# An adapter-merged linear layer: opening load ahead of the barrier, a held chunk, deeper turning, and set-up tensors inside a data buffer

## The chip, the cores and the metric

The kernel runs on one core of a Trainium2 chip. The metric is the device time of one launch in microseconds; the median of several runs is given. A profile of one execution shows what each engine did.

## What is computed

```python
x_flat = x.reshape(-1, in_dim)          # 32768 x 256, fp32
y = x_flat @ W                          # W: 256 x 256
lora_out = x_flat @ lora_A              # 256 x 16
lora_out = lora_out * lora_E            # 16
lora_out = lora_out @ lora_B            # 16 x 256
y = y + scale * lora_out
```

x and the output are 32 MB each. The low-rank part is merged into the weights once, so that per row of x there is one product with a 256 x 256 matrix.

## The kernel before

x is cut into 8 chunks of 4 MB. A chunk has 128 partitions with 32 rows of x on each, and sits in one of six buffers ("homes") in the on-chip memory. Results overwrite the x they come from, and the home is then stored. Chunks 6 and 7 reuse homes 0 and 1, so their loads (line 104, the wait in `load`) wait until chunks 0 and 1 are stored.

A chunk has 8 groups of 4 rows per partition; there are 64 groups, numbered through. Each passes these engines:

- GpSimd casts x to bf16 into `stage` (line 151), two buffers. It waits for the chunk's load where a chunk or piece begins, and for the turn two groups earlier.
- PE transposes the group in `turn` (line 196): pairs of bf16 are moved as fp32 words, four instructions a group, into `psum_xt`.
- ScalarE copies the turned x to `xt` (line 162), two buffers.
- PE multiplies by the merged weights in `multiply` (line 204), eight instructions a group, into `psum_y`.
- VectorE evicts `psum_y` to the home (line 181). After the last group of a chunk it signals that the chunk is done (line 185).

PE's program is a loop of `turn(i + 1)`, `multiply(i)`: it stands at the turn of the next group before it multiplies this one, so the last group of a chunk is multiplied only when the next chunk's first cast is there.

All transfers are issued by SyncE, in the order written out in `ORDER`: loads of chunks 0 to 5, stores of 0 and 1, loads of 6 and 7, stores of 2 to 7. The engines that move data take the transfers of a queue in this order. Chunk 0 is loaded in three pieces. After the first piece's load SyncE issues the four set-up loads (line 115: W, lora_A, lora_E, lora_B). A tiny store of 2 KB (line 125) goes out once the first group is evicted. Each store waits for its chunk (`s_chunk`). The final wait for the stores (line 238) is appended at the end of SyncE's program.

Set-up: PE transposes lora_A (line 216), VectorE scales it by lora_E into `ate` (line 167), PE multiplies by lora_B (line 222), VectorE adds W and writes `weff` in bf16 (line 177). At entry all engines meet in a barrier before the kernel's own instructions begin.

Of the kernel before, what the change touches and what calls it, by code (L numbers as in the profile page):

```python
# [7 lines left out]
P = 128  # L8
FP32 = mybir.dt.float32
# [6 lines left out]
N_HOMES = 6  # L16
# [6 lines left out]

EARLY_AFTER = 1

CG = 4
GPC = ROWS // CG
N_GROUPS = N_CHUNKS * GPC

NS, NX, NT, NY = 2, 2, 2, 2  # L30

UNROLL = 4

# [2 lines left out]
def kernel(  # L36
# [10 lines left out]
    nc = tc.nc  # L47
# [3 lines left out]
    M = out_flat.shape[1]  # L51
    R = lora_B.shape[0]
    KT = K // P
    assert N == N_CHUNKS * ROWS * P and K == M and KT == 2

    x_chunks = x_flat.rearrange("(c p b) k -> c p b k", p=P, b=ROWS)
    y_chunks = out_flat.rearrange("(c p b) m -> c p b m", p=P, b=ROWS)

    sbuf, psum, sem = nc.alloc_sbuf_tensor, nc.alloc_psum_tensor, tc.alloc_semaphore
    homes = [sbuf(f"home{h}", [P, ROWS, K], FP32) for h in range(N_HOMES)]  # L60
    stage = [sbuf(f"stage{i}", [P, CG, K], BF16) for i in range(NS)]
    xt = [sbuf(f"xt{i}", [P, CG, KT, P], BF16) for i in range(NX)]
    ident = sbuf("ident", [P, P], FP32)

    w_sb = sbuf("w_sb", [P, KT, M], FP32)
    a_sb = sbuf("a_sb", [P, KT, R], FP32)
    b_sb = sbuf("b_sb", [R, M], FP32)
    e_sb = sbuf("e_sb", [R, 1], FP32)
    ate = sbuf("ate", [R, KT, P], FP32)
    weff = sbuf("weff", [P, KT, M], BF16)  # L70
    psum_xt = [psum(f"psum_xt{i}", [P, CG, P], FP32) for i in range(NT)]
    psum_y = [psum(f"psum_y{i}", [P, CG, M], FP32) for i in range(NY)]

    pieces = []
    for c in range(N_CHUNKS):
        s = 0
# [3 lines left out]
    loaded = {pc: sem(f"loaded_{pc[0]}_{pc[1]}") for pc in pieces}  # L80
    set_up_loaded = {n: sem(f"loaded_{n}") for n in ("w", "a", "b", "e")}
    stored_of = {c: sem(f"stored_{c}") for c in range(N_CHUNKS - N_HOMES)}
    stored_rest = nc.alloc_semaphore("stored_rest")
    s_ident = sem("ident_made")
    s_pe_set_up = sem("pe_set_up")
    s_ate = sem("ate_made")
    s_stage = sem("staged")
    s_turned = sem("turned")
    s_xt = sem("xt_made")
    s_y = sem("multiplied")  # L90
    s_free = sem("y_free")
# [4 lines left out]
    def home(c):  # L96
        return homes[c % N_HOMES]

    sync, gpsimd, scalar, vector, tensor = nc.sync, nc.gpsimd, nc.scalar, nc.vector, nc.tensor

    def sync_program():
        def load(pc):
            c, s, e = pc
            if c >= N_HOMES:
                sync.wait_ge(stored_of[c - N_HOMES], 16)
            sync.dma_start(out=home(c)[:, s:e, :], in_=x_chunks[c, :, s:e, :]).then_inc(loaded[pc], 16)

        load(pieces[0])
        for name, to, of in (
            ("w", w_sb, W.rearrange("(q t) m -> q t m", t=KT)),  # L110
            ("a", a_sb, lora_A.rearrange("(q t) r -> q t r", t=KT)),
            ("e", e_sb, lora_E[:, None]),
            ("b", b_sb, lora_B),
        ):
            sync.dma_start(out=to[:], in_=of).then_inc(set_up_loaded[name], 16)
        for step in ORDER:
            c = int(step[1:])
            if step[0] == "L":
                for pc in pieces:
                    if pc[0] == c and pc != pieces[0]:  # L120
                        load(pc)
                if c == EARLY_AFTER:

                    sync.wait_ge(s_first, 1)
                    sync.dma_start(out=y_chunks[0, :16, 0, :32], in_=home(0)[:16, 0, :32]).then_inc(s_early, 16)
            else:
                sync.wait_ge(s_chunk, c + 1)
                if c == 0:
                    sync.wait_ge(s_early, 16)
                sync.dma_start(out=y_chunks[c], in_=home(c)[:]).then_inc(stored_of.get(c, stored_rest), 16)  # L130

    def gpsimd_program():
        gpsimd.memset(ident[:], 0.0).then_inc(s_ident, 1)  # L133
        gpsimd.wait_ge(s_ident, 1)
        gpsimd.affine_select(  # L135
            out=ident[:],
            in_=ident[:],
            compare_op=ALU.not_equal,
            fill=1.0,
            base=0,  # L140
            pattern=[[-1, P]],
            channel_multiplier=1,
        ).then_inc(s_ident, 1)
        for g in range(N_GROUPS):
            c, b = g // GPC, g % GPC * CG
            for pc in pieces:
                if pc[0] == c and pc[1] == b:
                    gpsimd.wait_ge(loaded[pc], 16)
            if g >= NS:
                gpsimd.wait_ge(s_turned, g - NS + 1)  # L150
            gpsimd.tensor_copy(out=stage[g % NS][:], in_=home(c)[:, b:b + CG, :]).then_inc(s_stage, 1)  # L151

        gpsimd.wait_ge(s_turned, N_GROUPS - NS + 1)
        gpsimd.drain().then_inc(s_stage, 1)

    def scalar_program():
        for g in range(N_GROUPS):
            scalar.wait_ge(s_turned, g + 1)
            if g >= NX:
                scalar.wait_ge(s_y, g - NX + 1)  # L160
            halves = psum_xt[g % NT][:].bitcast(BF16).rearrange("q b (p t) -> q b t p", t=KT)
            scalar.copy(out=xt[g % NX][:], in_=halves).then_inc(s_xt, 1)  # L162

    def vector_program():
        vector.wait_ge(set_up_loaded["e"], 16)
        vector.wait_ge(s_pe_set_up, 1)
        vector.tensor_scalar(  # L167
            out=ate[:],
            in0=psum_y[0][:R, :KT, :P],
            scalar1=e_sb[:],  # L170
            scalar2=float(scale),
            op0=ALU.mult,
            op1=ALU.mult,
        ).then_inc(s_ate, 1)
        vector.wait_ge(set_up_loaded["w"], 16)
        vector.wait_ge(s_pe_set_up, 2)
        vector.tensor_add(out=weff[:], in0=w_sb[:], in1=psum_y[1][:, :KT, :]).then_inc(s_free, NY)  # L177
        for g in range(N_GROUPS):
            c, b = g // GPC, g % GPC * CG
            vector.wait_ge(s_y, g + 1)  # L180
            vector.tensor_copy(out=home(c)[:, b:b + CG, :], in_=psum_y[g % NY][:]).then_inc(s_free, 1)  # L181
            if g == 0:
                vector.drain().then_inc(s_first, 1)
            if g % GPC == GPC - 1:
                vector.drain().then_inc(s_chunk, 1)

    def tensor_program():
        def take(s):
            tensor.wait_ge(s, 1).then_inc(s, -1)  # L189

        def turn(i):
            take(s_stage)

            words = stage[i % NS][:].bitcast(FP32)
            for b in range(CG):
                ins = tensor.transpose(psum_xt[i % NT][:, b, :], words[:, b, :], ident[:])  # L196
            ins.then_inc(s_turned, 1)

        def multiply(i):
            take(s_xt)  # L200
            take(s_free)
            for b in range(CG):
                for t in range(KT):
                    ins = tensor.matmul(  # L204
                        psum_y[i % NY][:, b, :],
                        xt[i % NX][:, b, t, :],
                        weff[:, t, :],
                        start=(t == 0),
                        stop=(t == KT - 1),
                    )  # L210
            ins.then_inc(s_y, 1)

        tensor.wait_ge(s_ident, 2)
        tensor.wait_ge(set_up_loaded["a"], 16)
        for t in range(KT):
            ins = tensor.transpose(psum_y[0][:R, t, :P], a_sb[:, t, :], ident[:])  # L216
        ins.then_inc(s_pe_set_up, 1)
        turn(0)
        tensor.wait_ge(set_up_loaded["b"], 16)
        tensor.wait_ge(s_ate, 1)  # L220
        for t in range(KT):
            ins = tensor.matmul(psum_y[1][:, t, :], ate[:, t, :], b_sb[:], start=True, stop=True)  # L222
        ins.then_inc(s_pe_set_up, 1)
        assert N_GROUPS % UNROLL == 0 and all(UNROLL % n == 0 for n in (NS, NX, NT, NY))
        with tensor.Fori(0, N_GROUPS // UNROLL):
            for i in range(UNROLL):
                turn(i + 1)
                multiply(i)

    with tc.tile_critical(no_gpsimd_drain=True):  # L230
        sync_program()
        gpsimd_program()
        scalar_program()
        vector_program()
        tensor_program()

    def wait_for_stores(nc):
        nc.sync.wait_ge(stored_rest, 16 * N_HOMES).then_inc(stored_rest, -16 * N_HOMES)

    nc.at_finalize(wait_for_stores)  # L240


# [33 lines left out]
```

## Time and profile before

| what | value |
|---|---|
| time, median of 3 runs | 163.35 us (163.25 to 163.46) |
| span of the profiled execution | 162.0 us |
| moved | HBM read 33.85 MB, written 33.56 MB, mean 416 GB/s |
| eviction, line 181 | 64 of 1225 ns |
| cast, line 151 | 64 of 1042 ns |
| copy of turned x, line 162 | 64 of 1012 ns |
| a whole load of 4 MB, issue to landing | 19.7 us median |
| a store of 4 MB, issue to landing | 43.3 us median |

The long times from issue to landing are mostly time in the queue behind older transfers. A row of the page that cuts the span into 40 slices shows one slice as about 4 us. Times within the profile count from the first instruction recorded; the device time is 1.3 us longer than the span.

### The profile page before, as it was taken

How to read it: one execution, taken by the hardware profiler on the slowest of the kernel's cores; microseconds unless marked ns; L12 is line 12 of the kernel's file. 1: busy time of each engine (PE TensorE's matmuls, PEld its weight loads, DVE VectorE, ACT ScalarE, POOL GpSimd, SP SyncE). 2: the span in 40 equal slices, each digit the busy share in tenths (PEclk: the TensorE clock that was granted, in tenths of full speed). 3: DMA queues.
4: the chain of work that ended last, by engine and by line, in shares of the span. 5: the costliest groups of instructions: out<-in, count | busy, mean ns of one | idle time of the engine just before them, and what ended most of it. 6: DMA issues, size and time to landing. Idle time of an engine off the chain costs nothing. (4 is left out here: it accounts for less than half of the span.)

```text
span 162.0 us, 2150 instructions
## 1 busy us (share of the span) xinstructions
PE 96.9 (60%) x778; PEld 80.1 (49%) x778; DVE 79.6 (49%) x66; ACT 66.1 (41%) x65; POOL 67.1 (41%) x70
## 2 busy tenths in 40 slices
PE   0399928999999999999900089999960000000000
PEld 0268817888888888888800068888840000000000
DVE  0116854888888888888830017888880000000000
ACT  3044725777767677777700026676720000000000
POOL 1455518777777677777200066677500000000000
PEclk9999999999999999999995558999995555555555
DMA  5999898999999997999999999999999999999992
GB/s 166 419 455 457 388 518 388 388 518 388 388 518 388 388 512 324 461 390 429 469 396 429 469 396 429 455 421 429 445 429 429 445 421 453 421 429 445 421 429 105
DMA packets 2979, 67.43 MB, mean 416 GB/s; under 512 B 528, under 2 KB 544, under 8 KB 672
## 3 DMA queue, kind: packets, MB, share of 16 engines
q1 hardware_dynamic: 2976, 67.41, 97.5%
q14 instruction: 3, 0.02, 0.0%
HBM read 33.85 MB, written 33.56 MB: 416 GB/s over the span
## 5 line engine op out<-in xcount | busy, mean ns | idle before, releaser
L181 DVE COPY home<-psum_y 128x1024 f32<-128x1024 f32 x64 | 78.4, 1225 | 31.9 <-PE psum_y L204 29.9
L151 POOL CAST stage<-home 128x1024 bf16<-128x1024 f32 x64 | 66.4, 1042 | 47.8 <-DMA home<-in_x_dram 26.0
L162 ACT COPY xt<-psum_xt 128x1024 bf16<-128x1024 bf16 x64 | 64.8, 1012 | 51.6 <-PE psum_xt L196 51.6
L204 PE MATMUL psum_y<-weff,xt 128*128 128x256 bf16 x512 | 68.4, 278 | 0.4
L204 PEld LDWEIGHTS psum_y<-weff,xt 128*128 128x128 bf16 x512 | 47.0, 99 | 14.4 <-issue 6.4
L196 PE MATMUL psum_xt<-ident,stage 128*128 128x128 f32 x260 | 41.1, 283 | 16.0 <-PEq L189 16.0
L196 PEld LDWEIGHTS psum_xt<-ident,stage 128*128 128x128 f32 x260 | 31.9, 147 | 18.1 <-issue 17.2
L216 PE MATMUL psum_y<-ident,a_sb 128*16 128x128 f32 x2 | 0.6, 394 | 6.6 <-DMA a_sb<-in_lora_A_dram 6.6
L167 DVE TENSOR_SCALAR ate<-psum_y,e_sb 16x256 f32<-16x256 f32 x1 | 0.5, 472 | 7.3 <-PE psum_y L216 7.3
L216 PEld LDWEIGHTS psum_y<-ident,a_sb 128*16 128x16 f32 x2 | 0.1, 90 | 6.6 <-issue 6.6
L222 PE MATMUL psum_y<-b_sb,ate 16*128 16x256 f32 x4 | 2.1, 670 | 0.0
L177 DVE TENSOR_TENSOR weff<-w_sb,psum_y 128x512 bf16<-128x512 f32 x1 | 0.7, 689 | 2.4 <-PE psum_y L222 2.4
L162 ACT ACT_TABLE_LOAD x1 | 1.3, 1283 | 0.9 <-SPq L230 0.9
L222 PEld LDWEIGHTS psum_y<-b_sb,ate 16*128 16x128 f32 x4 | 1.2, 319 | 0.5 <-issue 0.3
L133 POOL MEMSET ident<- 128x128 f32 x1 | 0.2, 206 | 0.5 <-SPq L230 0.5
L135 POOL TENSOR_SCALAR_AFFINE_SELECT ident<-ident 128x128 f32<-128x128 f32 x1 | 0.3, 293 | 0.2 <-POOL ident L133 0.2
L257 POOL MEMSET const-float32-0.0<- 128x1 f32 x1 | 0.1, 99 | 0.2 <-issue 0.2
L257 POOL MEMSET const-bfloat16-1.0<- 128x1 bf16 x1 | 0.1, 103 | 0.0
L257 POOL MEMSET const-uint8-127<- 128x1 uint8 x1 | 0.1, 103 | 0.0
L257 POOL MEMSET const-float32-1.0<- 128x1 f32 x1 | 0.1, 99 | 0.0
## 6 DMA issues: line engine op xcount, KB each, us to landing
out_dram<-home SPq DMA_DIRECT2D x8, 4096.0 KB, 43.3
home<-in_x_dram SPq DMA_DIRECT2D x7, 4096.0 KB, 19.7
home<-in_x_dram SPq DMA_DIRECT2D x2, 1024.0 KB, 5.0
home<-in_x_dram SPq DMA_DIRECT2D x1, 2048.0 KB, 9.7
w_sb<-in_W_dram SPq DMA_DIRECT2D x1, 256.0 KB, 4.9
a_sb<-in_lora_A_dram SPq DMA_DIRECT2D x1, 16.0 KB, 4.6
e_sb<-in_lora_E_dram SPq DMA_DIRECT2D x1, 0.1 KB, 4.4
b_sb<-in_lora_B_dram SPq DMA_DIRECT2D x1, 16.0 KB, 3.8
```

Source lines behind the costliest of these rows:

```text
L133: gpsimd.memset(ident[:], 0.0).then_inc(s_ident, 1)
L135: gpsimd.affine_select(out=ident[:], in_=ident[:], compare_op=ALU.not_equal, fill=1.0, base=0, pattern=[[-1, P]], channel_multiplier=1,).t ...
L151: gpsimd.tensor_copy(out=stage[g % NS][:], in_=home(c)[:, b:b + CG, :]).then_inc(s_stage, 1)
L162: scalar.copy(out=xt[g % NX][:], in_=halves).then_inc(s_xt, 1)
L167: vector.tensor_scalar(out=ate[:], in0=psum_y[0][:R, :KT, :P], scalar1=e_sb[:], scalar2=float(scale), op0=ALU.mult, op1=ALU.mult,).then_in ...
L177: vector.tensor_add(out=weff[:], in0=w_sb[:], in1=psum_y[1][:, :KT, :]).then_inc(s_free, NY)
L181: vector.tensor_copy(out=home(c)[:, b:b + CG, :], in_=psum_y[g % NY][:]).then_inc(s_free, 1)
L196: ins = tensor.transpose(psum_xt[i % NT][:, b, :], words[:, b, :], ident[:])
L204: ins = tensor.matmul(psum_y[i % NY][:, b, :], xt[i % NX][:, b, t, :], weff[:, t, :], start=(t == 0), stop=(t == KT - 1),)
L216: ins = tensor.transpose(psum_y[0][:R, t, :P], a_sb[:, t, :], ident[:])
L222: ins = tensor.matmul(psum_y[1][:, t, :], ate[:, t, :], b_sb[:], start=True, stop=True)
L257: nc = _bacc.Bacc("TRN2", target_bir_lowering=False, num_devices=1)
```

## The change

It does several things at once:

- The first x load and the load of lora_A are moved, after the program has been built, to the front of SyncE's and ScalarE's instructions, ahead of the entry barrier ("early load").
- The set-up loads are issued by ScalarE instead of SyncE, lora_A first and W last.
- W, lora_B, the scaled transposed lora_A and lora_A lie in the last home, home 5. The load of chunk 5 waits for the merged weights (`s_weff`) before it overwrites them.
- PE turns two groups ahead of the multiplication, with four buffers for turned x in PSUM and four in the on-chip memory.
- GpSimd's first cast of chunk 5 (the sixth chunk) waits until chunks 0 and 1 are stored ("held back as well": chunks 6 and 7 wait for these stores already, through their loads).
- The last signal of GpSimd counts two, for the two turns that run past the end; the callback that appends the final wait is registered earlier in the source.

The aim is to start the transfers sooner, to free memory for the buffers, and to keep compute of chunk 5 away from the first two stores.

```diff
+HELD = N_HOMES - 1
-NS, NX, NT, NY = 2, 2, 2, 2
+NS, NX, NT, NY = 2, 4, 4, 2
...
-    w_sb = sbuf("w_sb", [P, KT, M], FP32)
-    a_sb = sbuf("a_sb", [P, KT, R], FP32)
-    b_sb = sbuf("b_sb", [R, M], FP32)
+    last_home = homes[N_HOMES - 1]
+    w_sb = last_home[:, 0:KT, :]
+    b_sb = last_home[:R, KT, :]
+    ate = last_home[:R, KT + 1, :].rearrange("r (t p) -> r t p", p=P)
+    a_sb = last_home[:, KT + 2, :KT * R].rearrange("q (t r) -> q t r", r=R)
...
+    opening = []
+    def ahead_of_entry_barrier(nc):
+        blocks = nc.main_func.blocks
+        for name in opening:
...
+            first = blocks[0].instructions
+            at = next(
+                n for n, i in enumerate(first) if i.engine == ins.engine and isinstance(i, mybir.InstDrain)
+            )
+            blocks[0].instructions = first[:at] + [ins] + first[at:]
+    nc.at_finalize(ahead_of_entry_barrier)
...
     def sync_program():
         def load(pc):
             c, s, e = pc
+            if c == N_HOMES - 1:
+                sync.wait_ge(s_weff, 1)
...
-        load(pieces[0])
-        for name, to, of in (
...
-            sync.dma_start(out=to[:], in_=of).then_inc(set_up_loaded[name], 16)
+        opening.append(load(pieces[0]).ins.name)
...
+            if (c, b) == (HELD, 0):
+                for held_by in stored_of.values():
+                    gpsimd.wait_ge(held_by, 16)
...
-        gpsimd.drain().then_inc(s_stage, 1)
+        gpsimd.drain().then_inc(s_stage, 2)
...
     def scalar_program():
+        for name, to, of in (
+            ("a", a_sb, lora_A.rearrange("(q t) r -> q t r", t=KT)),
+            ("e", e_sb[:], lora_E[:, None]),
+            ("b", b_sb, lora_B),
+            ("w", w_sb, W.rearrange("(q t) m -> q t m", t=KT)),
+        ):
+            ins = scalar.dma_start(out=to, in_=of).then_inc(set_up_loaded[name], 16)
+            if name == "a":
+                opening.append(ins.ins.name)
...
+        vector.drain().then_inc(s_weff, 1)
...
+        turn(1)
...
             for i in range(UNROLL):
-                turn(i + 1)
+                turn(i + 2)
                 multiply(i)
```

More of the change, by code (lines that the diff above doesn't have):

```diff
@@ L63 @@
     ident = sbuf("ident", [P, P], FP32)
-    w_sb = sbuf("w_sb", [P, KT, M], FP32)
-    a_sb = sbuf("a_sb", [P, KT, R], FP32)
-    b_sb = sbuf("b_sb", [R, M], FP32)
+    last_home = homes[N_HOMES - 1]
[3 more added lines that the diff above has]
+    a_sb = last_home[:, KT + 2, :KT * R].rearrange("q (t r) -> q t r", r=R)
     e_sb = sbuf("e_sb", [R, 1], FP32)
-    ate = sbuf("ate", [R, KT, P], FP32)
     weff = sbuf("weff", [P, KT, M], BF16)
@@ L86 @@
     s_ate = sem("ate_made")
+    s_weff = sem("weff_made")
     s_stage = sem("staged")
@@ L99 @@
     sync, gpsimd, scalar, vector, tensor = nc.sync, nc.gpsimd, nc.scalar, nc.vector, nc.tensor
+    opening = []
+    def ahead_of_entry_barrier(nc):
+        blocks = nc.main_func.blocks
+        for name in opening:
+            block = next(b for b in blocks if any(i.name == name for i in b.instructions))
+            ins = next(i for i in block.instructions if i.name == name)
+            assert not ins.sync_info.on_wait
+            block.instructions = [i for i in block.instructions if i.name != name]
+            first = blocks[0].instructions
[4 more added lines that the diff above has]
+    nc.at_finalize(ahead_of_entry_barrier)
     def sync_program():
@@ L103, in load @@
             c, s, e = pc
+            if c == N_HOMES - 1:
+                sync.wait_ge(s_weff, 1)
             if c >= N_HOMES:
                 sync.wait_ge(stored_of[c - N_HOMES], 16)
-            sync.dma_start(out=home(c)[:, s:e, :], in_=x_chunks[c, :, s:e, :]).then_inc(loaded[pc], 16)
-        load(pieces[0])
-        for name, to, of in (
[L110 to L114, printed above, removed]
-            sync.dma_start(out=to[:], in_=of).then_inc(set_up_loaded[name], 16)
+            ins = sync.dma_start(out=home(c)[:, s:e, :], in_=x_chunks[c, :, s:e, :])
+            return ins.then_inc(loaded[pc], 16)
+        opening.append(load(pieces[0]).ins.name)
         for step in ORDER:
@@ L167, in vector_program @@
         vector.tensor_scalar(
-            out=ate[:],
+            out=ate,
             in0=psum_y[0][:R, :KT, :P],
@@ L176, in vector_program @@
         vector.wait_ge(s_pe_set_up, 2)
-        vector.tensor_add(out=weff[:], in0=w_sb[:], in1=psum_y[1][:, :KT, :]).then_inc(s_free, NY)
+        vector.tensor_add(out=weff[:], in0=w_sb, in1=psum_y[1][:, :KT, :]).then_inc(s_free, NY)
+        vector.drain().then_inc(s_weff, 1)
         for g in range(N_GROUPS):
@@ L221, in tensor_program @@
         for t in range(KT):
-            ins = tensor.matmul(psum_y[1][:, t, :], ate[:, t, :], b_sb[:], start=True, stop=True)
+            ins = tensor.matmul(psum_y[1][:, t, :], ate[:, t, :], b_sb, start=True, stop=True)
         ins.then_inc(s_pe_set_up, 1)
+        turn(1)
         assert N_GROUPS % UNROLL == 0 and all(UNROLL % n == 0 for n in (NS, NX, NT, NY))
@@ L226, in tensor_program, with wait_for_stores @@
             for i in range(UNROLL):
-                turn(i + 1)
+                turn(i + 2)
                 multiply(i)
+    def wait_for_stores(nc):
+        nc.sync.wait_ge(stored_rest, 16 * N_HOMES).then_inc(stored_rest, -16 * N_HOMES)
+    nc.at_finalize(wait_for_stores)
     with tc.tile_critical(no_gpsimd_drain=True):
@@ L235 @@
         tensor_program()
-    def wait_for_stores(nc):
-        nc.sync.wait_ge(stored_rest, 16 * N_HOMES).then_inc(stored_rest, -16 * N_HOMES)
-    nc.at_finalize(wait_for_stores)
 _INS = ['x', 'W', 'lora_A', 'lora_B', 'lora_E', 'scale']
```

## The prediction

> **What bounds the kernel now.** I read the page's lines on engines and queues first, then the clock and DMA rows, SyncE's own waits, and last a table of windows around the end.
>
> ```profile
> PE 96.9 (60%) x778; PEld 80.1 (49%) x778; DVE 79.6 (49%) x66; ACT 66.1 (41%) x65; POOL 67.1 (41%) x70
> PEclk9999999999999999999995558999995555555555
> DMA  5999898999999997999999999999999999999992
> q1 hardware_dynamic: 2976, 67.41, 97.5%
> ```
>
> No compute engine is busy over 60%, and PE is done three quarters through; the DMA row is full from the second slice to the last but one. The queue's share of 97.5% says that the 16 DMA engines together were at work for 0.975 x 162.0 = 158.0 us. The chain of waits names PE, but ends at 121 us with the last eviction, 41 us before the span does; it is not the bound.
>
> ```profile
> SPq L130 <- DVEq L185: 50.5, 5, 13.3
> SPq L106 <- DMA out_dram<-home: 43.5, 2, 34.0
> SPq L238 <- SPq L238: 39.0, 1, 39.0
> ```
>
> SyncE waits for compute (first row) and for two stores before it may refill homes (second), but in both cases older transfers are still queued. Its last 39.0 us are the wait for the stores. So the end is: time of the first byte, plus what the transfers take in line, plus what the slowest engine lags.
>
> ```profile
> 0.94 0.38 SPq L106 DMA_DIRECT2D home<-in_x_dram  x1
> 3.59 1.37 SPq L106 DMA_DIRECT2D home<-in_x_dram  x3
> ...
> 158.50:159.00 0.50, 0.00 (x0) 0.00 (x0) 0.00 (x0) 0.00 (x0) 0.00 (x0) 0.50 0.31 131
> 159.00:159.50 0.50, 0.00 (x0) 0.00 (x0) 0.00 (x0) 0.00 (x0) 0.00 (x0) 0.50 0.16 66
> 159.50:160.00 0.50, 0.00 (x0) 0.00 (x0) 0.00 (x0) 0.00 (x0) 0.00 (x0) 0.50 0.00 0
> 160.00:160.50 0.50, 0.00 (x0) 0.00 (x0) 0.00 (x0) 0.00 (x0) 0.00 (x0) 0.50 0.15 66
> ```
>
> The first load is issued at 0.94 us; in the trace's packet records its first data packet starts at 1.95 us, so 1.01 us later. At the other end (last two columns: DMA share, GB/s, packets counted where they start) one packet starts after 159.5 us: 0.15 of 16 engines x 0.5 us is 1.2 us, one 32 KB packet, of one engine.
>
> The packet records give the sum. A 32 KB packet takes 1.213 us (median of 1920), so a 4 MB chunk, 8 packets on each engine, takes 9.70 us, and 8 loads and 8 stores 155.3 us. The arrivals of each transfer (one per engine) give the lag. The median engine lands the last store at 159.45 us, the second last at 159.85, the last at 161.53. The last arrival moves on by 10.04 us in the store of chunk 1 (landing 82.51), 9.73 in the load of 6, 10.12 in that of 7, then in the stores 10.13 (chunk 2), 10.24 (3), 9.76 (4) and 9.68 from there. Against 9.68 that is 0.36, 0.05, 0.44, 0.45, 0.56, 0.08: 1.94 us. In those stretches one packet after the other on one engine takes 1.27 to 1.32 us; the first such run is from 64.6 to 80.0 us, the second from 104.8 to 122.7.
>
> The windows show what goes with it: the first run lies in stores with PE at work (to 81 us), the second likewise (PE to 120 us). From 13 to 59 us PE works beside loads, and after 123 us stores run alone; neither has slow packets. **Stores with compute beside them slow one engine**, about 0.07 us a packet.
>
> [...] the last wait ends 0.49 us after the 161.53 arrival, not after the median. [...] the lag appears in stores with compute alone, so I don't take it as constant. [...] clock 0.5 from 84.6 to 98.3 us, work restarting at 93.95.
>
> **The change, part by part.**
>
> *Opening load ahead of the entry barrier.* SyncE's first instruction is at 0.00 and it is held by the barrier to 0.66. The issue moves from 0.94 to about 0.00, the first byte from 1.95 to about 1.01: **0.94 us off**, all on the path, because transfers run on without a gap from there. Bounds: 0 (if the launch lets nothing flow sooner) to 0.94. I take 0.94. SyncE reaches the barrier 0.38 later and ScalarE, with an issue of 0.42, too; GpSimd's memsets keep the barrier to 0.54 anyhow, so it moves by some 0.1 us. Nothing in the DMA line waits for that.
>
> *Set-up loads on ScalarE.* Four issues leave SyncE (0.42 + 0.42 + 0.76 + 0.41 = 2.0 us), and the second x load goes out near 1.1 instead of 3.59. The first load occupies the engines for 3 us from its first byte in either case, so no gap closes: nothing gained. Their bytes stay. On ScalarE they end near 2.6, and the 1.28 us table load near 3.9, before the first turned x (8.09 now). Hidden. PE's set-up, which waited 6.6 us for lora_A, starts earlier, which nobody at the end waits for.
>
> *Tensors in the last home.* The load of chunk 5 now waits for the merged weights: made by 10.9 us, issue at 16.04. Behind it in SyncE are the stores; all free.
>
> *Turns two ahead, four buffers.* The period is 11.30 us for 8 groups, 1.41 each. PE needs 0.44 + 0.87 = 1.31 (chain rows), DVE 1.225 plus about 0.06: I take 1.31. Off the DMA path: nothing directly. The last two groups of a chunk now wait for the next chunk's casts, where one did (chunk 5 was finished at 98.0 instead of 82.5 for that). The stores have slack: store 5 reaches its turn at the engines only at 130, store 7 at 150.
>
> *Chunk 5 held until stores 0 and 1 have landed.* Behind GpSimd's wait stand all later casts, PE, and groups 38 and 39, so store 4. Groups 8 to 37 follow from 27 at 1.31: compute stops near 66. Stores 0 and 1 land near 81 (82.51 less 0.94 less 0.4). Then 26 groups remain: about 1.1 to the first turn, 4.6 us at half clock for 3.3 groups (as in the cold stretch now), 22.7 x 1.31 = 29.7: compute ends near 116.5, against 121.2. Load 6 (91) and load 7 (100) are there when turns 48 (94) and 56 (105) want them; store 4 is ready at 85 and starts at 119. So the hold puts no gap in the line, and its wait is free.
>
> What it removes is compute beside stores 0 and 1. Of the slow run in store 0, 7 packets x 0.07 = 0.5 us (an engine that was early at 62 us used it up, so the last arrival hid it), about 0.1 remains; of 0.36 in store 1, nothing; of 0.56 + 0.08 at stores 3 and 4, 0.45, since compute ends 4.7 us sooner. Loads 6 and 7 get more compute beside them, which by the stretch from 13 to 59 costs nothing; the 0.44 at load 7 and 0.45 at store 2 stay. Slow engine: 161.53 - (0.5 + 1.94) = 159.09 without lag; + 0.1 + 0.44 + 0.45 + 0.45 = 160.53; less 0.94 = 159.59. The others' latest is 159.85 - 0.94 = 158.91, so the slow one still ends it. Saving 161.53 - 159.59 = **1.94 us**: 163.35 - 1.94 = 161.4.
>
> *The moved final callback and the larger last increment* cost nothing: both lie where the stores are still under way.
>
> **Rivals.**
> *The lag goes with compute after 62 us, whatever transfer it meets.* Moved work then slows the engine beside loads 6 and 7. For it: load 7 lost 0.44. Against: load 6 only 0.05, earlier loads none. Only the early start counts: 163.35 - 0.94 = 162.4.
> *The slow engine drops behind the others altogether*, because denser compute ends earlier and the loss at load 7 belonged to that chunk's start. Then the rest set the end, 158.91: 163.35 - (161.53 - 158.91) = 160.7. Against: two stores still meet compute.
> *Slower.* The early issue brings nothing (lower bound, 0), the lag stays within 0.2, and another turn of direction costs what the first did: the load of chunk 5 took 10.55 us by its median arrival (52.02 to 62.57), 0.85 over 9.70, with PE at work; after the change PE restarts just as stores turn to loads at 81. 163.35 - 0.2 + 0.85 = 164.0. Against: the turns now at 82 and 101 move the median arrival by 9.68 and 9.71.
>
> **How the numbers follow.** Forecast 0.58, lag moved 0.24, others set the end 0.12, slower 0.06. The range runs from the case of 160.7 to just over that of 162.4, so 160.7 to 162.5; beyond it lie the slower case and a failed early start. Faster by over 0.2% (below 163.02): 0.93; within 0.2%: 0.02; slower: 0.05.
>
> **What would show it.** First DMA issue of SyncE at 0.0 and bytes in the window from 1.0 us; PE idle from about 66 to 82 at falling clock; no 1.28 us packets in stores 0 and 1; last arrival near 159.6, some 0.7 behind the second last. It is wrong if the packets beside loads 6 and 7 stretch, if a slice of the DMA row between 2 and 155 us falls below its present level, or if the first byte does not come sooner.

## The result and the profile after

The changed kernel takes 161.94 us (median of 4 runs, 161.79 to 162.47) against 163.36 us (4 runs, 163.25 to 163.46): a ratio of 0.9919, 95% interval 0.9894 to 0.9944. On another chip it was 162.05 against 163.56, 0.9897 (0.9869 to 0.9925). It is faster by about 0.9%; the forecast was 161.4 us, 1.2%.

The page of the changed kernel, the same rows as before:

```profile
PE 94.2 (59%) x782; PEld 83.9 (52%) x782; DVE 79.5 (50%) x66; ACT 66.0 (41%) x65; POOL 67.0 (42%) x70
...
PEclk9999999999999999955555999999998555555555
DMA  7999999999999999999999999999999999999993
...
q1 hardware_dynamic: 2624, 67.11, 97.9%
q10 hardware_dynamic: 352, 0.30, 0.5%
```

The bound is the same. The DMA row begins with 7 instead of 5, and the set-up tensors have a queue of their own (q10). The half-clock stretch of PE is longer: 20.5 us from 68.6 us, with PE at rest from 66.1 to 83.5 while stores 0 and 1 passed, against 13.7 us from 84.7 before, with PE at rest from 81.2 to 93.9. SyncE's waits in the changed kernel:

```profile
SPq L131 <- DMA out_dram<-home: 42.8, 2, 33.4
...
SPq L264 <- SPq L264: 36.6, 1, 36.6
```

SyncE still ends by waiting for stores and nothing else. Where the 1.5 us of span went is seen at both ends. First SyncE's own timeline, then windows of the changed kernel (last two columns DMA share and GB/s):

```profile
0.00 2.44 SPq L131 DMA_DIRECT2D home<-in_x_dram  x4
```

```profile
1.00:2.00 1.00, 0.00 (x0) 0.00 (x0) 0.00 (x0) 0.00 (x0) 0.50 (x2) 1.00 1.00 221
...
158.00:158.50 0.50, 0.00 (x0) 0.00 (x0) 0.00 (x0) 0.00 (x0) 0.00 (x0) 0.50 0.16 66
158.50:159.00 0.50, 0.00 (x0) 0.00 (x0) 0.00 (x0) 0.00 (x0) 0.00 (x0) 0.50 0.16 66
159.00:159.50 0.50, 0.00 (x0) 0.00 (x0) 0.00 (x0) 0.00 (x0) 0.00 (x0) 0.50 0.00 0
```

The data-moving engines are full from 1.0 us. In the packet records the first data packet starts at 1.00 us (1.95 before), and the median engine lands the last store at 158.51 us (159.45 before): 0.94 us earlier, kept to the end. No data packet starts after 159.0 us, where before one started after 160. The last arrival is at 159.95 us (161.53 before), 1.44 us behind the median engine instead of 2.08. So of the 1.58 us that the last arrival gained, **0.94 is the early start and 0.64 a smaller lag** (the distance from the median engine to the last).

Stage windows of the changed kernel (PE first, DMA last):

```profile
66.00:82.00 16.00, 0.12 (x2) 0.00 (x0) 1.30 (x2) 0.30 (x1) 0.00 (x0) 0.58 1.01 434
82.00:89.00 7.00, 5.50 (x26) 4.53 (x27) 1.33 (x2) 2.02 (x2) 4.10 (x4) 0.50 1.00 432
89.00:101.00 12.00, 12.00 (x112) 11.19 (x111) 10.92 (x9) 9.11 (x9) 9.33 (x9) 1.00 1.01 437
...
112.00:122.00 10.00, 8.72 (x80) 7.83 (x78) 9.44 (x8) 5.06 (x5) 3.12 (x3) 1.00 1.01 433
```

PE rests from 66 to 82 us, and the DMA share stays at 1.0 throughout: the hold opens no gap. But the seven microseconds after it run at half clock with two evictions, and compute reaches 122 us instead of the 116.5 forecast.

I counted stretched 32 KB packets: those over 1.24 and under 1.40 us where the normal one takes 1.213; excess is their time over that. The upper limit leaves out longer single packets, such as those of 1.41 to 2.03 us near 60 us in the profile before.

| kernel | 62 to 81 us (stores 0, 1): packets, excess | 101 to 125 us (stores 2, 3, start of 4) |
|---|---|---|
| before | 14, 1.04 us | 14, 1.06 us |
| changed | 3, 0.16 us | 17, 1.37 us |

The packets of one data-moving engine can also be followed in a row, since most start 3 or 4 ns before the recorded end of the one before (1679 of 1904 steps between 32 KB packets in the profile before). In the changed kernel's profile the engine that ends last is the one with the 17 stretched packets after 101 us: beyond 1.213 us a packet it lost 1.51 us after 62.5 us, 1.37 of it in them. In the profile before, the last engine lost at least 2.09 us there: 0.52 in stretched packets beside store 1, 1.06 in those after 101 us, and 0.41 in a single packet of 1.62 us at 100.7 us. No such packet fell on the last engine of the changed kernel's profile. So up to 0.41 of the 0.64 us can be that one packet, which is luck and not the hold.

### The profile page after: what moved, and what is told of

It is laid out like the page before. It is cut to its first block, busy times and chain, and to the rows that moved or that the text cites. A ratio compares the mean times of both kernels' runs of the same rounds, so it can differ in the third digit from the quotient of the medians.

```text
span 160.5 us, 2160 instructions
## 1 busy us (share of the span) xinstructions
PE 94.2 (59%) x782; PEld 83.9 (52%) x782; DVE 79.5 (50%) x66; ACT 66.0 (41%) x65; POOL 67.0 (42%) x70
## 5 line engine op out<-in xcount | busy, mean ns | idle before, releaser
L236 PE MATMUL psum_y<-weff,xt 128*128 128x256 bf16 x512 | 69.4, 281 | 2.6 <-PEq L221 2.5
L236 PEld LDWEIGHTS psum_y<-weff,xt 128*128 128x128 bf16 x512 | 51.4, 101 | 9.6 <-issue 3.2
L228 PE MATMUL psum_xt<-ident,stage 128*128 128x128 f32 x264 | 42.5, 287 | 18.6 <-PEq L221 18.6
L228 PEld LDWEIGHTS psum_xt<-ident,stage 128*128 128x128 f32 x264 | 33.1, 149 | 21.1 <-issue 20.2
L198 DVE TENSOR_SCALAR home<-psum_y,e_sb 16x256 f32<-16x256 f32 x1 | 0.5, 472 | 6.6 <-DMA e_sb<-in_lora_E_dram 6.6
L208 DVE TENSOR_TENSOR weff<-home,psum_y 128x512 bf16<-128x512 f32 x1 | 0.7, 689 | 5.9 <-DMA home<-in_W_dram 5.9
L248 PE MATMUL psum_y<-ident,home 128*16 128x128 f32 x2 | 0.6, 394 | 5.1 <-DMA home<-in_lora_A_dram 5.1
L254 PE MATMUL psum_y<-home 16*128 16x256 f32 x4 | 2.1, 670 | 0.2 <-DMA home<-in_lora_B_dram 0.2
L254 PEld LDWEIGHTS psum_y<-home 16*128 16x128 f32 x4 | 1.2, 319 | 0.8 <-DMA home<-in_lora_B_dram 0.6
## 6 DMA issues: line engine op xcount, KB each, us to landing
home<-in_W_dram ACTq DMA_DIRECT2D x1, 256.0 KB, 10.9
```

The lines of the kernel that those rows point to most:

```text
L198: vector.tensor_scalar(out=ate, in0=psum_y[0][:R, :KT, :P], scalar1=e_sb[:], scalar2=float(scale), op0=ALU.mult, op1=ALU.mult,).then_inc(s ...
L208: vector.tensor_add(out=weff[:], in0=w_sb, in1=psum_y[1][:, :KT, :]).then_inc(s_free, NY)
L236: ins = tensor.matmul(psum_y[i % NY][:, b, :], xt[i % NX][:, b, t, :], weff[:, t, :], start=(t == 0), stop=(t == KT - 1),)
L254: ins = tensor.matmul(psum_y[1][:, t, :], ate[:, t, :], b_sb, start=True, stop=True)
```

## The experiments

Ratios are to the kernel before, in runs on the same chip. "Lag" is last arrival less median arrival of the last store, from the packet records of one profiled execution. "Stretched" is what the engine that ended last lost in stretched packets after 62 us, at the least.

| kernel | time, us | ratio, 95% | less than before, us | lag, us | stretched, us |
|---|---|---|---|---|---|
| early start alone | 162.93 | 0.9950, 0.9933 to 0.9967 | 0.68 | 2.60 | 2.11 |
| hold alone | 162.80 | 0.9942, 0.9921 to 0.9963 | 0.81 | 1.35 | 1.36 |
| changed, no hold | 162.45 | 0.9920, 0.9896 to 0.9944 | 1.16 | 2.86 | 2.04 |
| changed, late start | 162.63 | 0.9938, 0.9916 to 0.9960 | 0.98 | 1.22 | 0 |
| changed, on a third chip | 162.05 | 0.9897, 0.9869 to 0.9925 | 1.51 | 1.75 | 0.07 |
| changed, no compute | 161.82 | 0.9867, 0.9812 to 0.9923 | 1.83 | 2.52 | 0 |
| W first, store 1 in halves | 171.51 | 1.0475, 1.0449 to 1.0502 | -7.95 | 1.75 | not followed |

### The early start alone

```diff
 (kernel before)
-        load(pieces[0])
+        opening.append(load(pieces[0]).ins.name)   # moved ahead of the entry barrier
```

> The kernel before with one edit: the first x load is issued ahead of the entry barrier. My theory (the end is first byte plus the line of transfers plus the lag of the slowest engine): first byte at 1.0 us instead of 1.95, lag as before, so 163.36 - 0.95 = 162.4 us, ratio 0.994. Rival, the early start matters only together with the set-up loads on ScalarE's queue: no change, 163.4. Rival, the whole gain of the changed kernel is the early start: 161.9.

The first data packet started at 1.02 us, and the time fell by 0.68 us, of the 0.95 expected; the interval, 0.54 to 1.10 us, holds both. Without a second queue the early start works, so the first rival falls; the whole gain of the changed kernel (1.4 to 1.5) it isn't, so the second falls too. In the profiled execution the median engine ended 0.71 us earlier (158.74), and the lag was 2.60 instead of 2.08.

### The hold alone

```diff
 (kernel before, GpSimd)
+            if (c, b) == (HELD, 0):
+                for held_by in stored_of.values():
+                    gpsimd.wait_ge(held_by, 16)
```

> The kernel before with one edit: the first cast of chunk 5 waits until chunks 0 and 1 are stored. My theory (stores with compute beside them slow one engine): no packets of 1.27 to 1.3 us while stores 0 and 1 pass, so the last arrival gains 0.3 to 0.9 us: about 162.8 us, ratio 0.996. Rival, the lag goes with the compute after 62 us wherever it lies: no change, 163.4.

162.80 us: the forecast figure. From 62 to 81 us it had 10 stretched packets instead of 14, where none was forecast; the last but one of them starts at 72 us, since with a period of 1.41 us compute of chunk 4 ran on to about there. The median engine ended no sooner than before (159.72 against 159.45), and the lag shrank to 1.35. So a lag moved along with the work is ruled out: the work moved beside loads 6 and 7 cost less than it had beside the stores. Together the two single edits give 0.68 + 0.81 = 1.49 us, as much as the whole change.

### The changed kernel without the hold

```diff
-            if (c, b) == (HELD, 0):
-                for held_by in stored_of.values():
-                    gpsimd.wait_ge(held_by, 16)
```

> The changed kernel without the hold of chunk 5. My theory: compute returns beside stores 0 and 1, the run of slow packets with it, and the last arrival moves back by 0.3 to 0.9 us: about 162.4 us, 0.5 above the changed kernel. Rival, all of the gain is the early start: 161.9, as the changed kernel.

162.45 us. Stretched packets from 62 to 81 us are back, 13 with 1.04 us of excess, and the last arrival is 161.58 us with a lag of 2.86; this profile is of the slowest of its six runs. Twelve of the 13 lie on the engine that ended last. So it is shown that the hold takes these packets away. Its size in time is 1.51 - 1.16 = 0.35 us by comparison with the changed kernel, across two chips and with intervals that overlap. On one and the same chip this kernel gained 0.48 us more than the early start alone, and neither has the hold; those intervals overlap too, so what the other edits add stays open.

### The changed kernel with the late start

```diff
-        opening.append(load(pieces[0]).ins.name)
+        load(pieces[0])
...
-            if name == "a":
-                opening.append(ins.ins.name)
```

> The changed kernel with both opening loads left behind the entry barrier. My theory: first byte at about 1.95 us, all else as in the changed kernel, so 161.94 + 0.95 = 162.9 us. Rival, the early start is given back by a later lag: 161.9 to 162.2.

162.63 us. First data at 1.94, the median engine at 159.58 against 158.51 in the changed kernel's profile: the start passes to the median end in full. The times differ by 1.51 - 0.98 = 0.53 us, with the same caution on chips. The lag is 1.22 here, 0.22 less than in the changed kernel's profile, which takes back a part. It is a lag of another kind: the last engine had no stretched packet in the two stretches and lost only 0.14 us after 62.5 us.

### No compute at all

The casts, turns, copies, products and evictions of all 64 groups are left out; VectorE only waits for each chunk's load and signals the chunk as done.

> The changed kernel with all work on the 64 groups left out (casts, turns, copies, products, evictions): x is loaded and stored unchanged, in the same order of transfers; the set-up stays. My theory: no packet of 1.27 to 1.3 us beside any store, all engines end within 0.4 us, the end at about 158.9 + 0.5 = 159.4 us of span, 160.7 us. Open: whether the 0.7 us that every engine loses near 60 us, where loads turn to stores, is there without compute too; if it goes, 160.0 us. Rival, the slow engine is slow by itself in stores: the run of slow packets is there, 161.5 us or more.

This one taught most. There is no run of stretched packets: none from 62 to 81 us and two after 101, against 3 and 17. So the run belongs to compute. Yet the median time is 161.82, hardly below the changed kernel. Its four runs spread widely: two (160.79 and 161.17) came near the 160.7 of the theory, two (162.48 and 162.58) did not, and the profile is of the slowest. Windows at its end (no ScalarE column, since it did nothing):

```profile
158.00:158.50 0.50, 0.00 (x0) 0.00 (x0) 0.00 (x0) 0.00 (x0) 1.00 0.16 66
...
159.50:160.00 0.50, 0.00 (x0) 0.00 (x0) 0.00 (x0) 0.00 (x0) 1.00 0.15 66
```

One packet starts more than a microsecond after all others, with no compute anywhere. The arrivals tell when the last one fell behind: 1.37 us behind the median when the second piece of chunk 0 landed (9 us), 2.32 at the load of chunk 5 (62 us), where a single packet took 2.84 us, 2.52 from load 7 on, and nothing after. The loss near 60 us, in the last packets of load 5, stays without compute too: that load took 10.28 us by the median engine.

So there are two kinds of lag, and which engine each falls on differs between executions. Where they fall on different engines, **the larger one sets the end**. In the changed kernel's profile that was the one of compute. In its profile on the third chip the two ended within 0.05 us of each other: the last engine, with hardly a stretched packet, 1.75 us behind the median, and the one with the stretched run 1.70. Where both fall on one engine they add up, as in the no-cast kernel below: its last engine was already 1.4 us behind when store 0 landed, and after the stretched run it ended 3.04 behind.

### Which work stretches the packets

Three kernels leave out work of one engine each, in one profiled execution each. In the first GpSimd signals without casting, from the third group on; in the second VectorE signals without evicting; in the third PE does one of four transposes and two of eight products per group. In the first two a drain stands in place of the work, so they test the work and not the number of these engines' instructions.

```diff
-            gpsimd.tensor_copy(out=stage[g % NS][:], in_=home(c)[:, b:b + CG, :]).then_inc(s_stage, 1)
+            if g < NS:
+                gpsimd.tensor_copy(...).then_inc(s_stage, 1)
+            else:
+                gpsimd.drain().then_inc(s_stage, 1)
```

```diff
-            vector.tensor_copy(out=home(c)[:, b:b + CG, :], in_=psum_y[g % NY][:]).then_inc(s_free, 1)
+            vector.drain().then_inc(s_free, 1)
```

```diff
 (in turn and in multiply)
-            for b in range(CG):
+            for b in range(1):
```

> The changed kernel without GpSimd's casts from the third group on: every group works on the first two staged groups. If GpSimd's traffic slows the one engine, the run of 1.27 to 1.3 us packets beside stores of chunks 2 and 3 goes, and the last arrival comes about 0.8 to 1.2 us sooner against the median one. If another engine does it, the run stays as in the changed kernel (13 to 18 packets).

> The changed kernel without VectorE's evictions: the loaded x is stored unchanged, everything ahead of the eviction runs. If VectorE's writes slow the one engine, the run of slow packets goes; if not, it stays, shorter by as much as compute ends sooner.

> The changed kernel with one of four transposes and two of eight products per group; the rest of the result comes from zeroed or old PSUM. Casts, copies and evictions stay at their full size. If PE's instructions (their number, or its reads) slow the one engine, the run of slow packets thins to about a quarter or goes; if the other engines do, it stays.

Then two kernels ask whether it is PE's data or its instructions.

```diff
-    psum_y[i % NY][:, b, :], xt[i % NX][:, b, t, :], weff[:, t, :]
+    psum_y[i % NY][:, b, :32], xt[i % NX][:, b, t, :], weff[:, t, :32]
```

```diff
+                for h in range(0, M, P):
                     for t in range(KT):
-                        psum_y[i % NY][:, b, :], ..., weff[:, t, :]
+                        psum_y[i % NY][:, b, h:h + P], ..., weff[:, t, h:h + P]
```

> The changed kernel with every product on 32 of the 256 output columns (the rest of the result is old PSUM): as many PE instructions, an eighth of the product's reads and writes. If the slow packets beside stores go with the number of PE instructions, the run stays (13 to 18 packets of 1.27 to 1.3 us after 101 us). If they go with the data that PE moves, it thins out.

> The changed kernel with each product split in two of 128 columns: the same data, 20 products and transposes a group instead of 12. If the slow packets go with the number of PE instructions, each is longer (0.13 us over 1.213 instead of 0.08) or more of them occur; if with the data, they stay at about 1.29 us. The period may grow with the added weight loads.

| kernel | time of the profiled run, us | stretched packets, 101 to 125 us | excess, us | median of the stretched, us |
|---|---|---|---|---|
| changed | 161.79 | 17 | 1.37 | 1.293 |
| no cast | 163.46 | 14 | 1.14 | 1.293 |
| no eviction | 162.28 | 18 | 1.56 | 1.293 |
| thin PE | 161.44 | 9 | 0.55 | 1.265 |
| narrow products | 161.62 | 12 | 1.03 | 1.293 |
| split products | 162.88 | 17 | 1.96 | 1.331 |
| no compute | 162.58 | 2 | 0.10 | 1.263 |

The times of single executions decide nothing here; the packets do.

That the edits did what they should is seen in the groups of instructions (name, form and count; then busy time and mean of one), for thin PE, narrow products and split products in turn:

```profile
L242 PE MATMUL psum_y<-weff,xt 128*128 128x256 bf16 x128 | 37.5, 396 | 14.9 <-PEq L227 14.4
```

```profile
L240 PE MATMUL psum_y<-weff,xt 128*128 128x32 bf16 x512 | 24.1, 182 | 5.5 <-PEq L225 5.4
```

```profile
L237 PE MATMUL psum_y<-weff,xt 128*128 128x128 bf16 x1024 | 71.3, 225 | 1.8 <-PEq L221 1.7
```

The stretched packet stays at 1.293 us without casts and without evictions. An eighth of the columns with as many instructions leaves it at 1.293. More instructions for the same products lengthen it to 1.331, and a quarter of them shorten it. For thin PE the count misleads: its compute ended at 114 us instead of 121 (narrow products at 115), and four packets of the run stay under 1.24 us. Taken in a row, its 11 packets from 101 us took 1.251 us in the mean, against 1.288 for the 16 of the changed kernel.

So the stretch goes with **how many instructions PE issues, and not with the width of the products**. It isn't proportional: 20 instructions a group instead of 12 gave 1.5 times the excess per packet (0.118 against 0.080 us). Two things are left. Each product has a weight load of its own (512 of each on line 236 of the changed kernel's page), so the number of instructions and the data read by weight loads rise and fall together in all these kernels and were not told apart. And a few packets stretch without PE's instructions: one or two of the packets counted in each kernel start just after the last store's issue, with PE at rest (issue at 122.06, packets at 122.26 and 123.58 us in the changed kernel); the two of the kernel without compute are of this sort. In what way an instruction of PE lengthens a packet isn't shown. Packets are seen only where a profile is taken, so whether they stretch without one isn't known.

### W first, and a hold that ends half-way

```diff
+        ins = sync.dma_start(out=w_sb, in_=...).then_inc(set_up_loaded["w"], 16)
+        opening.append(ins.ins.name)
         opening.append(load(pieces[0]).ins.name)
...
+                if c == 1:
+                    sync.dma_start(out=y_chunks[c, :64], in_=home(c)[:64]).then_inc(s_half, 16)
+                    sync.dma_start(out=y_chunks[c, 64:], in_=home(c)[64:]).then_inc(stored_of[c], 16)
+                    continue
...
-                for held_by in stored_of.values():
-                    gpsimd.wait_ge(held_by, 16)
+                gpsimd.wait_ge(stored_of[0], 16)
+                gpsimd.wait_ge(s_half, 16)
```

> The changed kernel with two edits: W is the first transfer, ahead of the barrier on SyncE (it landed at 12.9 us behind the x pieces), and the store of chunk 1 goes in two halves, the hold ending with the first one, so that PE restarts some 4 us sooner. Theory: merged weights near 8 us instead of 13.6, compute ends near 117 instead of 122, four packets fewer are slowed beside the store of chunk 3: 0.2 to 0.4 us below the changed kernel. Rival: the lag is set by what happens near 60 us and by which engine is hit, and nothing is gained: within 0.2 us.

It became much slower, for a reason in neither theory. Windows of this kernel around the halved store:

```profile
62.00:71.00 9.00, 4.51 (x42) 3.93 (x39) 5.44 (x5) 3.80 (x4) 1.86 (x2) 0.96 0.98 422
...
73.00:79.00 6.00, 0.00 (x0) 0.00 (x0) 0.00 (x0) 0.00 (x0) 0.00 (x0) 0.50 0.90 191
79.00:87.00 8.00, 5.09 (x24) 4.14 (x25) 1.23 (x1) 2.02 (x2) 4.11 (x4) 0.50 1.04 233
```

All 16 data-moving engines are busy (share 0.90 and 1.04), but move 191 and 233 GB/s instead of 422. The packets there take 2.55 us instead of 1.213. The two halves, each on 64 of the 128 partitions, kept all engines at work at about half the rate; why isn't shown. Over the run the excess packet time came to 9.6 us per engine, where the changed kernel had 0.95. The other edit did part of its work: the merged weights were begun at 9.86 us instead of 12.95. Neither it by itself nor a hold that ends sooner in another way was tried.

## Why the prediction was right, and where its steps were not

The direction, the bound and the range held: 161.94 lies between 160.7 and 162.5, on the slow side of 161.4. The steps below are compared with the profiled execution, 161.79, the fastest of the four.

- *Early start, 0.94 us*: right. First data packet at 1.00 us, median end 0.94 us sooner; alone, 0.71 at the median end and 0.68 us of time.
- *The hold puts no gap in the line*: right, DMA share 1.0 to 1.01 from 66 to 101 us.
- *Nothing in stores 0 and 1 any more*: right. Stretched packets 14 to 3, excess 1.04 to 0.16 us, where the prediction had 0.86 to 0.1.
- *Compute beside loads 6 and 7 costs nothing*: right. Of 220 packets from 82 to 98.5 us one took over 1.225 us, and the last arrival moved on by 9.68 and 9.76 us (store 1 at 81.77, load 6 at 91.45, load 7 at 101.21: in the order of the issues). The rival in which the lag moves along is out, since the hold alone gained what was forecast for it.
- *Compute ends near 116.5*: **wrong**, 122.0. The first turn came at 83.5, not 82.3, since store 1's last arrival came at 81.77 instead of 81.2 and GpSimd's wait ended 0.5 us after it, a step that the sum left out. PE then worked for 5.5 us at half clock and passed 2.2 groups, where I had 3.3 in 4.6 us: that figure is the length of the same stretch in the profile before over the full-speed period, while that stretch (93.95 to 98.56 us) holds 23 matmuls and transposes, under two groups. And the period in this part was 1.33 us, not 1.31. So the term "0.45 at stores 3 and 4 since compute ends sooner" came to 0.46 + 0.20 = 0.66 in the last arrival. In excess of stretched packets after 101 us it went up, 1.06 to 1.37, instead of down.
- *PE's set-up starts earlier*: lora_A did, by 1.5 us, but **W came later**. On ScalarE's queue it was issued at 1.99 us and landed 10.9 us after that, 4.9 before; its 2 KB packets are spread from 5.9 to 11.7 us among those of x, of 8 and 16 KB. The merged weights were begun at 12.95 us instead of 10.19. It cost nothing at the end, as the load of chunk 5 went out at 18.8 us, with its turn at the engines at 51. In the issues of transfers on the page of the changed kernel:

```profile
home<-in_W_dram ACTq DMA_DIRECT2D x1, 256.0 KB, 10.9
home<-in_lora_A_dram ACTq DMA_DIRECT2D x1, 16.0 KB, 4.9
```

- *The slow engine: 159.09 without lag, and 1.44 us of lag that stay*: **mis-sized, with errors that partly cancel.** The last engine's loss after 62.5 us was 1.51, close to 1.44, but made up otherwise: nothing beside stores 0 and 1 (0.1 forecast), no stalled packet at load 7 (0.44 forecast to stay), and 1.37 in stretched packets beside stores 2 to 4 (0.45 + 0.45 forecast). That the totals agree is luck. The larger miss is in the base: 159.09 lies 0.36 before the median engine's 159.45, while the last engine of the changed kernel, without its loss, ends at 158.44, only 0.07 before its median. So the last arrival came at 159.95 instead of 159.59, and the lag shrank by 0.64 where I gave it 1.00.
- *The lag appears in stores with compute alone*: **too narrow**. The kernel without compute has a lag of 2.52 us in its profile. In the changed kernel's profile, too, an engine was 0.79 us behind the median when load 5 landed, ahead of any whole-chunk store. There it did no harm: it ended second last, at 159.30, still 0.79 behind. One sum along one engine can't foretell the end where each of two lags may fall on any engine.
- *Turns two ahead*: the period fell from 1.41 to 1.31 (chunk to chunk at full clock in the first half, 10.5 us), as forecast. What it did for the end stays open: this edit was not run by itself, the single edits' sum of 1.49 us leaves little for it, and the 0.48 us by which the changed kernel without the hold beat the early start alone leaves room.

What stays open: which engine falls behind in the first loads and near 60 us, and why its loss differs between executions. It can be as large as what the hold removes, and may be why six runs of the changed kernel spread over 0.9 us.

## What to carry to other kernels

When transfers bound a kernel, look at three things apart: the first byte, the line of packets, and how far the last of the 16 engines trails the median one; windows of half a microsecond at the end show the last. What the issue moved ahead of the entry barrier gained at the first packet passed to the end for the most part (alone, 0.71 of 0.93 us at the median engine, and 0.68 of the time). Whether the faster compute loop was worth anything there isn't shown. Before a lag is put down to what runs beside it, run the transfers alone: here it separated a lag that goes with compute (17 stretched packets after 101 us with it, 2 without) from another that doesn't (2.52 us without it). Then follow the engine that ends last back in time, for the engine that was last in the middle need not be the one.

## What the runs showed of the hardware that I had not expected

- In stores, 32 KB packets of one engine take mostly 1.27 to 1.30 us instead of 1.213 while PE is issuing, and 1.32 to 1.35 with two thirds more PE instructions and weight loads. Without casts, without evictions and with products of an eighth of the width the median stayed at 1.293 us. Beside loads there is no such run: of 594 packets that start from 13 to 58 us in the kernel before, with PE at work, none took over 1.225 us.
- While the store of chunk 1 went out in two halves of 64 partitions, 191 to 233 GB/s were moved against 422 in the window ahead of it, with all 16 engines busy (shares of 0.90 and 1.04) and packets of 2.55 us instead of 1.213.
- In 13 of the 14 profiles the engines lose some 0.5 to 0.9 us once in the last packets of load 5, near 60 us (10.16 to 10.55 us for that load by the median engine instead of 9.7), with or without compute. In the changed kernel without the hold that load took 9.71, and a stall of about the same size stood near 4 us, in packets of the first loads of 1.05 to 1.41 us instead of 0.31. So the turn from loads to stores, which comes at the same place there, isn't shown to be its cause.
